# A decoder step on one core: the second mixer's score products 128 keys wide instead of 64

## The chip, the cores and the metric

The kernel runs on one core of one Trainium2 chip. The metric is the device time of one execution in microseconds (us): 1040.94 us, the median of three runs (1039.25 to 1043.57). The engines are TensorE (PE for its matmuls, PEld for its weight loads), VectorE (DVE), ScalarE (ACT), GpSimd (POOL) and SyncE (SP), which issues the DMAs. TensorE runs at one of two clock levels, 1.2 or 2.4 GHz; the profile gives it as a share of full speed.

## The reference

One inference step of a two-layer decoder: 256 prompt tokens and 8 sample tokens, 1024 channels. In each layer four recurrent mixers run side by side, then cross attention, then a feed-forward block. The change touches only the second mixer (HGRN2), and only its prompt part. For each of four heads of 64 channels it computes, in chunks of 64 tokens:

```
b     = cumsum(log_f)                     # per channel, along the tokens
A_ts  = sum_k q[t,k] * exp(b[t,k] - b[s,k]) * k[s,k]     for s <= t, else 0
o     = A @ v  +  (q * exp(b)) @ S        # S is the state carried over chunks
```

The decay between query t and key s is a product of the forget gates of all tokens between them, and it differs per channel.

## The kernel before

Nearly all of TensorE's work is dense projections: `dense` (L294 to L296) multiplies 264 token columns by 128x128 weight blocks in a split precision, three products a block: wh by xh, wh by xl, wl by xh. Weights come from HBM as 512 KB tiles `raw` on SP's queue; ACT makes `wh` (L230), DVE makes `wl` (`sub`, recorded at L92). TensorE takes its instructions in the order that the tile scheduler gave them; the mixers' small products are woven between the dense ones: the mixers are generators, each `yield` hands over to the next one, and one dense projection is put in between by the pace `PACE`.

In `hgrn` keys `hk` (K) and queries Q (a tile of the projection's, `PH` in the profile) lie with channels on the partitions: two heads share the 128 partitions (the halves `HS`: partitions 0 to 63 and 64 to 127), and `i` runs over four pairs of head pair and 128-token half. The matrix A is built in levels w = 1, 2, 4, 8, 16, 32. At level w the keys of each even block of w tokens meet the queries of the odd block that follows it. The key and query rows are scaled in place from level to level (two `mul`, `hk<-hk,hpr` and `PH<-PH,hpr`), so a product at level w already holds the right decays. `quads` issues the products (L740): for each of 4 `i`, 2 blocks of 64 keys (`a`) and 2 heads (`e`), one matmul of 64 keys by 32 queries, contracted over 64 channels. It thus lies in a quarter of the 128x128 array, 64 rows by 64 columns, and the four of one `i` lie in four different quarters. Each float32 matmul is two matmul records in the profile, each with its own weight load: 32 records a level. Before the levels `quads` makes the diagonal with 64 by 64.

The results of head `e` go to the PSUM buffer `ps[e]` (tag `pb`, two buffers, both in use at once). A masked copy on DVE (`copy_predicated`, L763, mask `h{w}`) puts those that belong to the level into `hAc`, 64 tokens wide; the diagonal is a `mul` with `h0`. After the levels `cross` (L772) makes the step across 64 (keys 0 to 63 by queries 64 to 127, 8 products of 64 by 64), and the final tiles `hAt` (one a head, 128 keys by 4 by 128 queries) are put together: a `memset` on DVE (L793), and six copies on ACT (L794, L796). The products with `hAt` (L814) give the output.

Of the kernel before, what the change touches and what calls it, by code (L numbers as in the profile page):

```python
# [10 lines left out]
U32 = mybir.dt.uint32  # L11
# [4 lines left out]
DEPTH, DM, TP, NB, NT = 2, 1024, 256, 8, 264  # L16
# [16 lines left out]
def build_consts():  # L33
    p = np.arange(128)
    cols, off, n = [], {}, 0

    def add(name, a):
        nonlocal n
        a = np.asarray(a, np.float32).reshape(128, -1)
        off[name] = (n, a.shape[1])  # L40
        n += a.shape[1]
        cols.append(a)

    add("ident", np.eye(128))
    add("blk64", (p[:, None] // 64) == (p[None] // 64))
    t64 = np.arange(64)
    s64 = (p % 64)[:, None]
    add("msi", np.concatenate([t64[None] > s64, t64[None] >= s64], 1))
    add("mh", np.stack([(p // 32) % 2 == 0, (p // 32) % 2 == 1], 1))
    t32 = np.arange(32)  # L50
    s32 = (p % 32)[:, None]
    add("id32", t32[None] == s32)
    for w in (1, 2, 4, 8, 16):
        add(f"inv{w}", ((t32[None] // w) % 2 == 1) & (s32 // w == t32[None] // w - 1))
    add("h0", t64[None] == s64)
    for w in (1, 2, 4, 8, 16, 32):
        t = t64[t64 // w % 2 == 1][None]
        add(f"h{w}", s64 // w == t // w - 1)
    add("mneg", np.where(p[None] >= p[:, None], 0.0, -1e30))
    add("pick", (p % 32)[:, None] == np.arange(4)[None])  # L60
    add("eye8", np.broadcast_to(np.eye(8), (128, 8, 8)))
    add("nsc", np.where(p < 32, -2.0, np.where(p < 64, 0.0, -1.0)))
    add("sgn", np.where(p >= 64, -1.0, 1.0))
    return np.ascontiguousarray(np.concatenate(cols, 1)), off


CONSTS, COFF = build_consts()


def body(tc, A, O, depth=DEPTH):  # L70
    nc = tc.nc
    V, S, P, PE = nc.vector, nc.scalar, nc.gpsimd, nc.tensor
# [18 lines left out]
    def tt(out, a, b, op):  # L91
        return V.tensor_tensor(out, a, b, op=op)  # L92

    def mul(out, a, b):
        return tt(out, a, b, ALU.mult)

    def add(out, a, b):
        return tt(out, a, b, ALU.add)
# [19 lines left out]
    def T(tag, shape, name, dt=F32):  # L118
        return wk.tile(list(shape), dt, tag=tag, name=name, bufs=NBUF[tag])

    def psum(tag, shape, name="pm"):
        return psp.tile(list(shape), F32, tag=tag, name=name, bufs=PBUF[tag])

    def tiny(shape, name, bufs=1):
        return wk.tile(shape, F32, tag=name, name=name, bufs=bufs)

    class Stream:
# [5 lines left out]
        def s2(self, name, shape=(128, 2, NT)):  # L133
            return T(self.big, shape, name)
# [7 lines left out]
        def pst(self, shape, name="pm"):  # L142
            return psum(self.ps, shape, name)
# [34 lines left out]
    for _ in range(WARM):  # L178
        ps = psum("pc", [128, 128], "warm")
# [5 lines left out]
    def C(name):  # L185
        o, n = COFF[name]
        return cst[:, o:o + n]

    ident, blk64 = C("ident"), C("blk64")
# [3 lines left out]
    HS = [slice(0, 64), slice(64, 128)]  # L193
# [477 lines left out]
    def hgrn(l, pv, PH):  # L671
        s2, s1, h5, pst, headsum = SB.s2, SB.s1, SB.h5, SB.pst, SB.headsum
        q, f, iv, g = PH
# [48 lines left out]
        def rows(src, t):  # L722
            S.copy(t, turned(pst, src))
            return t
# [1 line left out]
        yield  # L726
        Vr = rows(iv, s2("hVr", [128, 2, 256]))
        yield
        Ac = s2("hAc", [128, 2, 4, 64])
        K = kx[:, :, 0:TP]  # L730
        Q = f[:, :, 0:TP]

        def quads(cols, n):

            ps = [pst([128, 4, n]) for _ in HS]
            for i in range(4):
                for a, as_ in enumerate(HS):
                    t0 = i % 2 * 128 + a * 64
                    for e, hs in enumerate(HS):
                        PE.matmul(ps[e][as_, i, :], lhsT=K[hs, i // 2, t0:t0 + 64], rhs=cols(hs, i // 2, t0),  # L740
                                  start=True, stop=True)
            return ps

        ps = quads(lambda hs, j, t0: q[hs, j, t0:t0 + 64], 64)
        mul(Q, q[:, :, 0:TP], fx[:, :, 0:TP])
        for e in range(2):
            mul(Ac[:, e], ps[e], C("h0")[:, None, :].to_broadcast([128, 4, 64]))
        tw, prod, o = fx[:, :, 0:TP], T("B", [128, 2 * NT], "hpr"), 0
        for w in (1, 2, 4, 8, 16, 32):
            yield  # L750
            ng = TP // (2 * w)
            halves = lambda t: t.rearrange("p j (g two w) -> p j g two w", two=2, w=w)
            ps = quads(lambda hs, j, t0: Q[hs, j, t0:t0 + 64].rearrange("p (g two w) -> p g two w", two=2, w=w)[:, :, 1], 32)
            tv = tw.rearrange("p j (g two) -> p j g two", two=2)
            tn = prod[:, o:o + 2 * ng].rearrange("p (j g) -> p j g", j=2)
            o += 2 * ng
            mul(tn, tv[:, :, :, 0], tv[:, :, :, 1])
            for t, c in ((K, 0), (Q, 1)):
                mul(halves(t)[:, :, :, c], halves(t)[:, :, :, c],
                    tv[:, :, :, 1 - c, None].to_broadcast([128, 2, ng, w]))  # L760
            by = lambda t: t.rearrange("p c (g w) -> p c g w", w=w)
            for e in range(2):
                V.copy_predicated(Ac[:, e].rearrange("p c (g two w) -> p c g two w", two=2, w=w)[:, :, :, 1],  # L763
                                  by(C(f"h{w}")[:, None]).to_broadcast([128, 4, 32 // w, w]).bitcast(U32), by(ps[e]))
            tw = tn

        def cross():
            ps = pst([128, 4, 64])
            for i in range(4):
                t0 = i % 2 * 128  # L770
                for hs in HS:
                    PE.matmul(ps[hs, i, :], lhsT=K[hs, i // 2, t0:t0 + 64], rhs=Q[hs, i // 2, t0 + 64:t0 + 128],  # L772
                              start=True, stop=True)
            return ps

        yield
        if l == 0:
            held.append(Q[:, 0, 0:1])
        psD = cross()
        n = TP // 128  # L780
        qv = Q.rearrange("p j (n two w) -> p j n two w", two=2, w=64)
        kv = K.rearrange("p j (n two w) -> p j n two w", two=2, w=64)
        tv = tw.rearrange("p j (n two) -> p j n two", two=2)
        tn = tiny([128, 2, n], "htw64")
        mul(kv[:, :, :, 0], kv[:, :, :, 0], tv[:, :, :, 1:2].to_broadcast([128, 2, n, 64]))
        mul(qv[:, :, :, 1], qv[:, :, :, 1], tv[:, :, :, 0:1].to_broadcast([128, 2, n, 64]))
        mul(tn, tv[:, :, :, 0], tv[:, :, :, 1])
        tw = tn
        yield
        Kr = rows(K, q.rearrange("p j t -> p (j t)")[:, 0:2 * TP].rearrange("p (c d) -> p c d", c=2))  # L790
        At = [s2("hAt", [128, 4, 128]) for _ in HS]
        for e, hs in enumerate(HS):
            V.memset(At[e][64:128, :, 0:64], 0.0)  # L793
            S.copy(At[e][0:64, :, 64:128], psD[hs])  # L794
            for as_ in HS:
                S.copy(At[e][as_, :, as_], Ac[as_, e])  # L796
        yield
        psG = pst([128, 4, 64])
        for i in range(4):
# [11 lines left out]
        for i in range(4):  # L811
            j, c = i // 2, i % 2
            for h, hs in enumerate(HS):
                PE.matmul(psO[hs, i, :], lhsT=Vr[:, c, j * 128 + h * 64:j * 128 + h * 64 + 64], rhs=At[h][:, i, :],  # L814
                          start=True, stop=c == 0)
# [662 lines left out]
    def layer(l):  # L1478
# [97 lines left out]
        def chain_b():  # L1576
            yield from hgrn(l, pv, PH)
            for _ in d_ml:
                pass
            yield from mlstm(l, pv, PQ, sp, y)  # L1580
# [97 lines left out]
    g = PVL[0]["final_norm_g"]  # L1678
# [7 lines left out]
    t = [SA.s2("y") for _ in range(4)]  # L1686
# [130 lines left out]
```

## Time and profile before

| | |
|---|---|
| median of three runs | 1040.94 us |
| the profiled execution's own time | 1044.91 us |
| its span, first to last instruction | 1043.1 us |
| TensorE busy | 1026.8 us, 98% |
| VectorE busy | 791.7 us, 76% |
| ScalarE busy | 630.5 us, 60% |
| mean granted TensorE clock | 0.988 |

The span is what the profile covers; 1.8 us of the execution lie around it. The profiled execution is 4.0 us longer than the median of the others. A busy share is an average over stages; which engine bounds a stage is read from the waits in it. The mixers of the first layer run from about 25 to 230 us, those of the second from about 540 to 740 us.

### The profile page before, as it was taken

The numbers are of one execution on the slowest core, as the hardware profiler recorded it, in microseconds if no ns is written. First come the engines' busy times: TensorE is split into PE (matmuls) and PEld (weight loads), VectorE is DVE, ScalarE is ACT, GpSimd is POOL, SyncE is SP. The second block draws the span as 40 slices with busy tenths as digits, with TensorE's granted clock in tenths as the row PEclk, the third lists the DMA queues.
The fourth block names the chain that finished last, engine by engine and source line by source line (L and its number), as shares of the span: only waits on it lengthen the run. The fifth ranks groups of instructions, "written<-read, shape, count | busy, mean of one in ns | idle before, by whom it ended". The sixth has DMA issues, their size and how long they took to land.

```text
span 1043.1 us, 26569 instructions
## 1 busy us (share of the span) xinstructions
PE 1026.8 (98%) x10522; PEld 967.6 (93%) x10522; DVE 791.7 (76%) x1766; ACT 630.5 (60%) x1345; POOL 43.4 (4%) x71
## 2 busy tenths in 40 slices
PE   9999999999999999999999999999999999999996
PEld 8999899989879999999999999998988899999996
DVE  7989587688578777868669776876886787777763
ACT  7865456476457766644569354746664577775443
POOL 0000000002002000000010000000020020000000
PEclk9999989999999999999999999999999999999998
DMA  8664267588884566678654433756969655667782
GB/s 283 187 205 125 86 152 232 191 285 281 296 306 154 180 182 182 186 240 289 219 179 153 140 119 116 214 191 210 325 197 340 233 180 179 180 177 225 224 261 79
DMA packets 81580, 213.42 MB, mean 205 GB/s; under 512 B 16432, under 2 KB 19120, under 8 KB 81456
## 3 DMA queue, kind: packets, MB, share of 16 engines
q1 hardware_dynamic: 81456, 211.72, 63.6%
q8 instruction: 83, 1.36, 0.5%
q14 instruction: 41, 0.34, 0.1%
HBM read 195.81 MB, written 15.87 MB: 203 GB/s over the span
## 4 chain that ended last, share of the span: by engine, by line
PE 93%; DVE 4%; ACT 2%; issue 1%; DMA 0%; POOL 0%; DVEq 0%; SPq 0%; ACTq 0%
PE pd L294 21%; PE pd L296 20%; PE pd L295 20%; PE pm L1365 3%; PE pd L307 3%; PE pd L309 2%; PE pd L308 2%; PE pd L1318 2%; PE pd L1319 1%; DVE wl L92 1%; PE pm L1454 1%; PE pd L1320 1%; PE pm L344 1%; PE pm L149 1%; PE pm L1429 1%
## 5 line engine op out<-in xcount | busy, mean ns | idle before, releaser
L230 ACT CAST wh<-raw 128x512 fp32r<-128x512 f32 x544 | 335.9, 619 | 264.0 <-PE pd L295 224.2
L92 DVE TENSOR_TENSOR wl<-raw,wh 128x512 fp32r<-128x512 f32 x544 | 379.1, 700 | 140.0 <-ACT wh L230 125.9
L294 PE MATMUL pd<-xh,wh 128*128 128x264 f32 x1136 | 332.9, 293 | 0.2 <-ACT xh L89 0.2
L295 PE MATMUL pd<-xl,wh 128*128 128x264 f32 x1136 | 326.6, 287 | 0.4 <-DVE xl L110 0.4
L296 PE MATMUL pd<-xh,wl 128*128 128x264 f32 x1136 | 326.4, 287 | 0.2 <-DVE wl L92 0.2
L294 PEld LDWEIGHTS pd<-xh,wh 128*128 128x128 f32 x1136 | 216.5, 191 | 6.4 <-issue 2.2
L296 PEld LDWEIGHTS pd<-xh,wl 128*128 128x128 f32 x1136 | 217.1, 191 | 1.5 <-DVE wl L92 1.1
L295 PEld LDWEIGHTS pd<-xl,wh 128*128 128x128 f32 x1136 | 216.7, 191 | 1.0 <-DVE xl L110 0.6
L294 PE MATMUL pd<-hid,wh 128*128 128x264 f32 x512 | 145.9, 285 | 0.0
L295 PE MATMUL pd<-hid,wh 128*128 128x264 f32 x512 | 145.6, 284 | 0.0
L296 PE MATMUL pd<-hid,wl 128*128 128x264 f32 x512 | 145.6, 284 | 0.0
L295 PEld LDWEIGHTS pd<-hid,wh 128*128 128x128 f32 x512 | 96.6, 189 | 0.0
L296 PEld LDWEIGHTS pd<-hid,wl 128*128 128x128 f32 x512 | 96.4, 188 | 0.0
L294 PEld LDWEIGHTS pd<-hid,wh 128*128 128x128 f32 x512 | 96.3, 188 | 0.0
L107 POOL TENSOR_TENSOR nacc<-nacc,nsq 128x264 f32<-128x264 f32 x41 | 36.7, 896 | 934.4 <-ACT nsq L89 654.7
L92 DVE TENSOR_TENSOR xT<-xT,pd 128x264 f32<-128x264 f32 x80 | 34.0, 424 | 14.2 <-PE pd L309 8.2
L110 DVE SCALAR_TENSOR_TENSOR fft<-pd,rstd 128x264 f32<-128x264 f32 x64 | 27.7, 432 | 15.2 <-PE pd L296 14.2
L1319 PE MATMUL pd<-wl,mgh 128*128 128x256 f32 x128 | 36.5, 286 | 1.3 <-DVE wl L92 1.3
L294 PE MATMUL pd<-mgh,wh 128*128 128x256 f32 x128 | 37.3, 291 | 0.0
L308 PE MATMUL pd<-ol,wh 128*128 128x264 f32 x128 | 37.2, 291 | 0.0
L307 PE MATMUL pd<-oh,wh 128*128 128x264 f32 x128 | 36.7, 289 | 0.5 <-ACT oh L1413 0.5
L1318 PE MATMUL pd<-wh,mgh 128*128 128x256 f32 x128 | 36.7, 292 | 0.0
(551 smaller groups left out, 1777.9 us busy)
## 6 DMA issues: line engine op xcount, KB each, us to landing
raw<-in_ff SPq DMA_DIRECT2D x128, 512.0 KB, 4.3
raw<-in_w_in SPq DMA_DIRECT2D x63, 512.0 KB, 3.7
KV<-in_ck SPq DMA_DIRECT2D x64, 256.0 KB, 5.3
KV<-in_cv SPq DMA_DIRECT2D x64, 256.0 KB, 4.9
raw<-in_wk SPq DMA_DIRECT2D x16, 512.0 KB, 3.5
raw<-in_wv SPq DMA_DIRECT2D x16, 512.0 KB, 4.7
raw<-in_w_out SPq DMA_DIRECT2D x16, 512.0 KB, 4.7
raw<-in_wq SPq DMA_DIRECT2D x16, 512.0 KB, 4.9
```

The lines of the kernel that those rows point to most:

```text
L92: return V.tensor_tensor(out, a, b, op=op)
L107: return P.tensor_tensor(out, a, b, op=ALU.add)
L110: return V.scalar_tensor_tensor(out, in0=a, scalar=s, in1=b, op0=op0, op1=op1, **kw)
L230: S.copy(h, src)
L294: PE.matmul(ps, lhsT=wh, rhs=x, start=i * 8 + k == 0, stop=False)
L295: PE.matmul(ps, lhsT=wh, rhs=y, start=False, stop=False)
L296: PE.matmul(ps, lhsT=wl, rhs=x, start=False, stop=i * 8 + k == n - 1)
L307: PE.matmul(ps, lhsT=wh, rhs=h[k], start=k == 0, stop=False)
L308: PE.matmul(ps, lhsT=wh, rhs=lo[k], start=False, stop=False)
L1318: PE.matmul(ps[m], lhsT=x[:, ms], rhs=wh[:, k % 2], start=first, stop=False)
L1319: PE.matmul(ps[m], lhsT=x[:, ms], rhs=wl[:, k % 2], start=False, stop=False)
L1365: PE.matmul(ps[g:g + 8, :], lhsT=lhs[:, hh, i, b * 8:b * 8 + 8], rhs=kv[a][hh][:, i], start=b < 2 and i == 0, stop=b >= NB - 2 and i == 1)
```

## The change

`quads` drops the loop over `a`: the stationary operand is now all 128 keys of a half, and one matmul is 128 keys by 64 queries (the odd blocks of 128 tokens), contracted over the 64 channels of its head. It lies in half of the array, 64 rows by all 128 columns. There are 8 matmuls a level instead of 16 (16 records instead of 32). The masks `h{w}` are 128 by 64, so the part of a product that belongs to another block is not copied. The masked copies write straight into the final tiles `At`, with 256 elements a partition instead of 128. The diagonal is 128 by 128 with the identity as its mask, which also writes the zeros. The step across 64 is a seventh level of the loop; `cross`, the two memsets and the six ACT copies a layer go. The constants' DMA grows from 1032 to 1224 columns.

```diff
-    add("h0", t64[None] == s64)
-    for w in (1, 2, 4, 8, 16, 32):
-        t = t64[t64 // w % 2 == 1][None]
-        add(f"h{w}", s64 // w == t // w - 1)
+    for w in (1, 2, 4, 8, 16, 32, 64):
+        t = p[p // w % 2 == 1][None]
+        add(f"h{w}", p[:, None] // w == t // w - 1)
...
-        Ac = s2("hAc", [128, 2, 4, 64])
+        At = [s2("hAt", [128, 4, 128]) for _ in HS]
...
-                for a, as_ in enumerate(HS):
-                    t0 = i % 2 * 128 + a * 64
-                    for e, hs in enumerate(HS):
-                        PE.matmul(ps[e][as_, i, :], lhsT=K[hs, i // 2, t0:t0 + 64], rhs=cols(hs, i // 2, t0),
-                                  start=True, stop=True)
+                t0 = i % 2 * 128
+                for e, hs in enumerate(HS):
+                    PE.matmul(ps[e][:, i, :], lhsT=K[hs, i // 2, t0:t0 + 128], rhs=cols(hs, i // 2, t0),
+                              start=True, stop=True)
...
-            mul(Ac[:, e], ps[e], C("h0")[:, None, :].to_broadcast([128, 4, 64]))
+            mul(At[e], ps[e], ident[:, None, :].to_broadcast([128, 4, 128]))
-        for w in (1, 2, 4, 8, 16, 32):
+        for w in (1, 2, 4, 8, 16, 32, 64):
...
-            ps = quads(lambda hs, j, t0: Q[hs, j, t0:t0 + 64].rearrange("p (g two w) -> p g two w", two=2, w=w)[:, :, 1], 32)
+            ps = quads(lambda hs, j, t0: Q[hs, j, t0:t0 + 128].rearrange("p (g two w) -> p g two w", two=2, w=w)[:, :, 1], 64)
...
-                V.copy_predicated(Ac[:, e].rearrange("p c (g two w) -> p c g two w", two=2, w=w)[:, :, :, 1],
-                                  by(C(f"h{w}")[:, None]).to_broadcast([128, 4, 32 // w, w]).bitcast(U32), by(ps[e]))
+                V.copy_predicated(At[e].rearrange("p c (g two w) -> p c g two w", two=2, w=w)[:, :, :, 1],
+                                  by(C(f"h{w}")[:, None]).to_broadcast([128, 4, 64 // w, w]).bitcast(U32), by(ps[e]))
...
-        psD = cross()
...
-        At = [s2("hAt", [128, 4, 128]) for _ in HS]
-        for e, hs in enumerate(HS):
-            V.memset(At[e][64:128, :, 0:64], 0.0)
-            S.copy(At[e][0:64, :, 64:128], psD[hs])
-            for as_ in HS:
-                S.copy(At[e][as_, :, as_], Ac[as_, e])
```

On TensorE, in the first layer around level w = 4, this stands before (operands as in the profile; x16 is a run of 16 matmuls of one line):

```order
L379 MATMUL pm<-cst,a 128x128 x4
L294 MATMUL pd<-xh,wh 128x264
L295 MATMUL pd<-xl,wh 128x264
L296 MATMUL pd<-xh,wl 128x264
L294 MATMUL pd<-xh,wh 128x264
L295 MATMUL pd<-xl,wh 128x264
L296 MATMUL pd<-xh,wl 128x264
L294 MATMUL pd<-xh,wh 128x264
L740 MATMUL pm<-PH_508,hk 64x32 x16
L295 MATMUL pd<-xl,wh 128x264
```

And the same place of the changed kernel, whose lines stand one or two numbers lower:

```order
L378 MATMUL pm<-cst,a 128x128 x4
L293 MATMUL pd<-xh,wh 128x264
L294 MATMUL pd<-xl,wh 128x264
L295 MATMUL pd<-xh,wl 128x264
L293 MATMUL pd<-xh,wh 128x264
L294 MATMUL pd<-xl,wh 128x264
L295 MATMUL pd<-xh,wl 128x264
L293 MATMUL pd<-xh,wh 128x264
L294 MATMUL pd<-xl,wh 128x264
L738 MATMUL pm<-PH_508,hk 128x64 x8
```

The group of 16 has become a group of 8, one dense matmul later; it is the only place on TensorE where a group stands elsewhere than before. In both layers all 16 groups (the diagonal, the six levels and `cross`, now the seventh level) keep their places between the others.

On DVE, in the second layer from level w = 8 on (`wl` and `PQ` belong to dense projections), before:

```order
L763 COPY_PREDICATED hAc<-cst,pm 128x16x8
L92 TENSOR_TENSOR hk<-hk,hpr 128x2x16x8
L92 TENSOR_TENSOR PH_8241<-PH_8241,hpr 128x2x16x8
L763 COPY_PREDICATED hAc<-cst,pm 128x16x8
L92 TENSOR_TENSOR wl<-raw,wh 128x512
L92 TENSOR_TENSOR PQ_8247<-pd,rstd 128x264
```

And of the change:

```order
L761 COPY_PREDICATED hAt<-cst,pm 128x32x8
L91 TENSOR_TENSOR hk<-hk,hpr 128x2x16x8
L91 TENSOR_TENSOR PH_8178<-PH_8178,hpr 128x2x16x8
L761 COPY_PREDICATED hAt<-cst,pm 128x32x8
L91 TENSOR_TENSOR wl<-raw,wh 128x512
L91 TENSOR_TENSOR PQ_8183<-pd,rstd 128x264
```

The masked copies stand where they stood and take twice the elements; the scaling of keys and queries between them is as before.

## Rows read from the trace of the kernel before

**Rows 1.** The page: engines' busy us, clock by slice, weight DMAs (KB, us to landing).

```profile
PE 1026.8 (98%) x10522; PEld 967.6 (93%) x10522; DVE 791.7 (76%) x1766; ACT 630.5 (60%) x1345; POOL 43.4 (4%) x71
...
PEclk9999989999999999999999999999999999999998
...
raw<-in_w_in SPq DMA_DIRECT2D x63, 512.0 KB, 3.7
```

**Rows 2.** Waits of PE: who, for what, us in total, times, longest.

```profile
PE pm L571 <- issue: 2.4, 1, 2.4
```

**Rows 3.** Stretches: length; busy us of PE, PEld, DVE, ACT, POOL; clock, DMA.

```profile
78.00:90.00 12.00, 11.86 (x216) 11.22 (x210) 12.00 (x36) 6.20 (x15) 0.00 (x0) 1.00 0.46 137
...
606.00:622.00 16.00, 16.00 (x335) 15.14 (x335) 11.88 (x34) 8.70 (x19) 0.00 (x0) 1.00 0.36 111
```

**Rows 4.** PE's timeline: start, us, tile, shape, records; two groups, each with its successor.

```profile
608.55 0.67 PE L740 MATMUL pm<-PH,hk 64*64 64x32 f32 x32
609.14 0.39 PE L294 MATMUL pd<-xh,wh 128*128 128x264 f32 x1
...
621.19 0.68 PE L772 MATMUL pm<-PH,hk 64*64 64x64 f32 x16
621.80 0.39 PE L294 MATMUL pd<-xh,wh 128*128 128x264 f32 x1
```

**Rows 5.** PE's timeline: groups of other weight widths and columns, each with its successor.

```profile
60.35 2.03 PE L344 MATMUL pm<-rRV,SWT 64*64 64x2 f32 x64
62.31 0.39 PE L294 MATMUL pd<-xh,wh 128*128 128x264 f32 x1
...
69.25 1.09 PE L534 MATMUL pm<-AR,a 64*64 64x128 f32 x16
70.28 0.29 PE L322 MATMUL pm<-cst,vec 128*48 128x128 f32 x1
...
162.47 1.06 PE L1187 MATMUL pm<-lgw,lKr 128*128 128x4 f32 x8
163.46 0.69 PE L1178 MATMUL pm<-lKr,lVg 128*64 128x64 f32 x14
...
181.74 0.92 PE L1221 MATMUL pm<-PQ,PQ 64*128 64x256 f32 x8
182.59 0.44 PE L859 MATMUL pm<-cst,RT 128*128 128x128 f32 x2
```

**Rows 6.** Line 1187's matmuls: duration in ns, min/median/max, first and last start.

```profile
L1187 PE MATMUL pm<-lgw,lKr x16: 252/253/273, 162.5 to 675.7; 128*128 128x4 f32 x16
```

**Rows 7.** Groups by shape: count, busy us, mean ns of one, idle before.

```profile
L763 DVE COPY_PREDICATED hAc<-cst,pm 128x128 f32<-128x128 uint32 x24 | 7.4, 349 | 0.9 <-PE pm L740 0.8
L92 DVE TENSOR_TENSOR M<-pm,cst 128x512 f32<-128x512 f32 x8 | 5.5, 685 | 1.9 <-PE pm L534 1.9
L92 DVE TENSOR_TENSOR hAc<-pm,cst 128x256 f32<-128x256 f32 x4 | 1.5, 414 | 0.0
L793 DVE MEMSET hAt<- 64x256 f32 x4 | 1.1, 272 | 0.4
...
L796 ACT COPY hAt<-hAc 64x256 f32<-64x256 f32 x8 | 3.2, 404 | 1.2 <-DVE hAc L763 1.0
```

**Rows 8.** Timeline of DVE, then of PE, around level w = 4, second layer.

```profile
603.61 0.44 DVE L763 COPY_PREDICATED hAc<-cst,pm 128x128 f32<-128x128 uint32 x1
...
604.55 0.43 DVE L763 COPY_PREDICATED hAc<-cst,pm 128x128 f32<-128x128 uint32 x1
...
604.78 1.00 PE L740 MATMUL pm<-PH,hk 64*64 64x32 f32 x32
605.71 0.39 PE L294 MATMUL pd<-xh,wh 128*128 128x264 f32 x1
```

**Rows 9.** Two stretches of the first layer, columns as in rows 3.

```profile
117.00:119.30 2.30, 0.00 (x0) 0.00 (x0) 0.00 (x0) 0.00 (x0) 0.00 (x0) 1.00 0.15 39
119.70:123.10 3.40, 3.40 (x16) 2.75 (x17) 0.00 (x0) 1.60 (x3) 0.00 (x0) 0.50 0.02 5
```

More of the change, by code (lines that the diff above doesn't have):

```diff
@@ L736, in quads @@
             for i in range(4):
-                for a, as_ in enumerate(HS):
-                    t0 = i % 2 * 128 + a * 64
-                    for e, hs in enumerate(HS):
-                        PE.matmul(ps[e][as_, i, :], lhsT=K[hs, i // 2, t0:t0 + 64], rhs=cols(hs, i // 2, t0),
-                                  start=True, stop=True)
+                t0 = i % 2 * 128
+                for e, hs in enumerate(HS):
+                    PE.matmul(ps[e][:, i, :], lhsT=K[hs, i // 2, t0:t0 + 128], rhs=cols(hs, i // 2, t0),
+                              start=True, stop=True)
             return ps
-        ps = quads(lambda hs, j, t0: q[hs, j, t0:t0 + 64], 64)
+        ps = quads(lambda hs, j, t0: q[hs, j, t0:t0 + 128], 128)
         mul(Q, q[:, :, 0:TP], fx[:, :, 0:TP])
         for e in range(2):
-            mul(Ac[:, e], ps[e], C("h0")[:, None, :].to_broadcast([128, 4, 64]))
+            mul(At[e], ps[e], ident[:, None, :].to_broadcast([128, 4, 128]))
         tw, prod, o = fx[:, :, 0:TP], T("B", [128, 2 * NT], "hpr"), 0
-        for w in (1, 2, 4, 8, 16, 32):
+        for w in (1, 2, 4, 8, 16, 32, 64):
             yield
@@ L762, in hgrn @@
             for e in range(2):
-                V.copy_predicated(Ac[:, e].rearrange("p c (g two w) -> p c g two w", two=2, w=w)[:, :, :, 1],
-                                  by(C(f"h{w}")[:, None]).to_broadcast([128, 4, 32 // w, w]).bitcast(U32), by(ps[e]))
+                V.copy_predicated(At[e].rearrange("p c (g two w) -> p c g two w", two=2, w=w)[:, :, :, 1],
+                                  by(C(f"h{w}")[:, None]).to_broadcast([128, 4, 64 // w, w]).bitcast(U32), by(ps[e]))
             tw = tn
[L767 to L776, printed above, removed]
         if l == 0:
             held.append(Q[:, 0, 0:1])
-        psD = cross()
[L780 to L788, printed above, removed]
         yield
         Kr = rows(K, q.rearrange("p j t -> p (j t)")[:, 0:2 * TP].rearrange("p (c d) -> p c d", c=2))
-        At = [s2("hAt", [128, 4, 128]) for _ in HS]
-        for e, hs in enumerate(HS):
-            V.memset(At[e][64:128, :, 0:64], 0.0)
-            S.copy(At[e][0:64, :, 64:128], psD[hs])
-            for as_ in HS:
-                S.copy(At[e][as_, :, as_], Ac[as_, e])
         yield
```

## The prediction

> **What bounds the kernel now.** Start with the page: TensorE (PE) is busy 1026.8 of 1043.1 us [rows 1], so only 16.3 us of the whole span are idle, and a gain or a loss elsewhere counts only if it reaches PE. Next read PE's waits: the longest is a single stop of 2.4 us [rows 2] in which PE waited for nothing that the profile shows. Then take the stretches where the second mixer's levels lie. In the first layer's 78 to 90 us PE is busy 11.86 of 12.00 and DVE 12.00; in the second's 606 to 622 us PE 16.00 of 16.00, DVE 11.88 and ACT 8.70 [rows 3]. There PE runs one instruction after the other, dense products around small ones. So what the change does to PE's own time there lengthens or shortens the kernel by the same amount; DVE matters only through a delay, above all at the start, where it has no slack; ACT does not matter.
>
> **What one group costs PE now.** I take start to next start, so that the array's switch between tile sizes is included. A level of 32 records (16 products of 64 keys by 32 queries, four quarters of the array side by side, so 8 rounds) takes 609.14 - 608.55 = 0.59 us; the cross step, 16 records of 64 by 64 queries, two quarters side by side, so also 8 rounds, takes 0.61 [rows 4]. Half the records and twice the columns, yet the same time: neither the count of instructions nor the columns set it. What is the same in both is the round's weights, 64 columns wide. L344 says so too: 64 records with 2 columns each, 32 rounds of two, take 1.96 us [rows 5]. With a fixed part S and a round p: 32p + S = 1.96 and 8p + S = 0.60 give p = 0.057 us and S = 0.15 us. A round lasts 0.057 us with 2, 32 or 64 moving columns: it waits for its weights of 64 columns.
>
> **What it costs then.** The new product has 128 weight columns and 64 moving ones; two (the two heads) lie side by side, so a level is again 8 rounds. For weights of 128 columns with hardly any moving ones there is L1187: 8 records, one after the other, 4 columns each, take 0.99 us [rows 5]; less S that is 0.105 us a round, and from its duration, (1.06 - 0.253) / 7, it is 0.115 [rows 5, 6]. That is twice the 0.057 of 64 columns. Do two such loads run side by side? L1221 is the same tile as the new one (64 rows, 128 columns, heads alternating): 8 records, two rounds of 256 and two of 128 columns, 0.85 us. L534 gives the price of moving columns: 8 rounds of 128 columns, 1.03 us, so 0.110 a round, 0.220 for 256. Two of each and S are 0.81; one product after the other would be 1.47. They run side by side [rows 5].
>
> So a new group is 8 x (0.105 to 0.115) + 0.15 = 0.99 to 1.07, I take 1.02, against 0.60: **+0.42 us a group**. The diagonal has 128 moving columns, 0.110 a round, and comes out the same; its old form had 32 records of 64 by 64 in four quarters, 8 rounds, 0.60. There are 8 groups a layer (the diagonal, six levels, the cross step that is now the seventh level), 16 in all: 16 x 0.42 = **+6.7 us**. From below: if a round stayed at 0.057 (64 moving columns alone need 0.055, half of L534's), only the two diagonals would grow, by 8 x 0.053 each: +0.9. From above: rounds that load and multiply in turn, 0.112 + 0.055 = 0.167 with 64 columns and 0.222 with the diagonal's 128: 14 x (1.49 - 0.60) + 2 x (1.93 - 0.60) = +15.
>
> The row's verdict can be set against a rule. The Trainium skill, "TensorE: Matmul & The Clock Gate", section "The mechanism", says that a weight load overlaps products in flight only where the row group differs. By it the next pair's weights could not load under this pair's products, and the sum would be the upper end just worked out. Here L772 speaks against it: by that rule its group would be 8 x (0.057 + 0.055) + 0.15 = 1.05, and it is 0.61 [rows 4].
>
> **DVE.** The masked copies go from 24 of 128 elements, 0.349 us each, to 28 of 256. The trace has no such copy of 256; a product from PSUM takes 0.414 with 256 and 0.685 with 512 elements [rows 7], so 128 more cost 0.135 (bounds: nothing, if the fixed part is all, and 0.27), and I take 0.484. That is 28 x 0.484 - 24 x 0.349 = +5.2; the four diagonal products go from 0.414 to 0.685, +1.1; the four memsets, 1.1 in all, go. Sum +5.2 us over both layers. Nearly all of it lies beside PE, which is itself 6.7 longer in the same stretches; in 78 to 90 us DVE gets about +0.5 for the diagonal and 6 x 0.135 for three levels, 1.3, and PE there four groups, 1.7, so the copies still fit. If that cover were gone, 5.2 us would be the price.
>
> One place is not covered. At level w = 4 PE's group follows the previous one after a few dense products and takes 605.71 - 604.78 = 0.93 instead of 0.59: its second head waits for the PSUM buffer until the second copy of level w = 2 is done (604.55 + 0.43 = 604.98) [rows 8]. Behind it queue the dense products. Two longer copies lie ahead of that release, 2 x 0.135 = 0.27 a layer: **+0.5 us** over both (0 to 1.1). In the first layer one dense matmul now stands ahead of the group, which can only shorten this wait.
>
> **The rest.** The six ACT copies a layer (0.404 each for four of them [rows 7]) end long before L814 needs their tiles, and ACT is half idle: 0. The seventh level brings one pair of copies behind the scaling of the keys, whose transposes stand a dense projection later: 0. The constants' DMA has 98 KB more ahead of weight tiles on SP's queue, a fifth of a tile that lands in 3.7 us [rows 1], 0.7 us; PE's list of waits has none for a DMA, so 0, and 0.7 if that cover is gone.
>
> **Sum.** +6.7 + 0.5 = +7.2 us. On the profiled execution's own time, 1044.91 us (span 1043.1 and 1.8 around it), that is 1052.1. This execution lies 4.0 us above the median of 1040.94, perhaps by the stop below; on the median the sum is 1048.1, and I forecast 1048 us.
>
> **Rivals.** A, a round stays at 0.057, since two row halves load one under the other: +0.9 + 0.5, 1042.3 us. For it: no row shows 128-column weights in two halves with as few as 64 moving columns. Against: L1187 and the doubling from 64 to 128.
>
> B, on the other side: the count of PE's instructions decides. A level's 0.45 us without S is 0.0141 a record; with half the records twelve levels lose 0.225 each, -2.7, the diagonals still need +0.9. And the stop: from 117.0 to 119.3 us no engine does anything, in the middle of a group of 64 tiny products, and then PE runs at the lower clock level, 1.2 GHz (0.50), for 3.4 us [rows 9], 1.7 lost, part of the first dip in the page's clock line [rows 1]. If PE lacks instructions there, the 224 fewer of them a layer (112 products and 112 loads) could end it, -4.1. Together -5.9: 1035.0 us. It decides if a level's group takes clearly less than 0.59. Against: 16 records of L772 take as long as 32 of L740 [rows 4]. The Trainium skill, "TensorEngine Tiling (Array Packing)", section "Instruction Overhead", speaks for it: about 60 cycles a matmul whatever its columns. An estimate by it, 25 ns at 2.4 GHz, makes 0.8 us of the old level; the trace has 0.59.
>
> C, the forecast's PE cost, but the stop falls away since the instructions stand elsewhere, and the median holds it: 1048.1 - 4.1 = 1044 us. For: nothing in the profile explains the stop; against: the second layer has the same code and no such stop.
>
> D, load and product in turn: +15 + 0.5, 1056.4 us.
>
> **Chances.** Forecast 0.66, A 0.12, B 0.05, C 0.11, D 0.06. A measurement of this kernel tells 0.5%, 5.2 us, from no change: faster is below 1035.7, slower above 1046.1. Faster: B, 0.05. Same: A, C and the forecast's lower edge, 0.26. Slower: the rest, 0.69. The range 1042 to 1053 holds the forecast with its bounds (0.99 to 1.07 a group and 0 to 1.1 of waiting make 1047.2 to 1049.6, and the runs themselves spread by 4.3), A and C; B and D are left out.
>
> **What would show it.** PE's groups of the new line: about 1.02 us from start to next start, 16 records each; at 0.60 it is A, below 0.5 B, near 1.5 D. The copies at 256 elements near 0.48 us, the group at w = 4 some 0.27 longer than the others plus the 0.34 it waits now, all else in these stretches unchanged and PE still without idle time. The forecast is wrong if the groups don't lengthen, or if they do and the end doesn't move with them.

## The result, and the profile after

The changed kernel takes 1056.57 us (median of four runs, 1053.78 to 1058.74) against 1042.26 of the kernel before beside it (four runs): a ratio of 1.013, interval 1.0098 to 1.0162. That is slower, as forecast, but by 14.3 us instead of 7.2, and outside the range.

The profiled execution has a span of 1056.8 us and a mean granted clock of 0.984. Its page, engines and clock by slice:

```profile
PE 1038.3 (98%) x10298; PEld 977.2 (92%) x10298; DVE 799.3 (76%) x1766; ACT 625.5 (59%) x1333; POOL 43.7 (4%) x71
...
PEclk9989889999999999999999999999999999999998
```

TensorE is busy 11.5 us longer with 224 matmul records less [rows 1]. The levels of the second mixer, PE's timeline (columns as in [rows 4]): the diagonal and w = 4 in the first layer, then w = 4 and w = 8 in the second, each with its successor.

```profile
81.64 1.16 PE L738 MATMUL pm<-PH,hk 64*128 64x128 f32 x16
82.73 0.39 PE L293 MATMUL pd<-xh,wh 128*128 128x264 f32 x1
...
94.38 1.64 PE L738 MATMUL pm<-PH,hk 64*128 64x64 f32 x16 [0.23 <-DVE hAt L761]
95.95 0.40 PE L295 MATMUL pd<-xh,wl 128*128 128x264 f32 x1
...
616.23 1.70 PE L738 MATMUL pm<-PH,hk 64*128 64x64 f32 x16 [0.19 <-DVE PH L91]
617.86 0.39 PE L293 MATMUL pd<-xh,wh 128*128 128x264 f32 x1
...
620.68 1.11 PE L738 MATMUL pm<-PH,hk 64*128 64x64 f32 x16
621.72 0.39 PE L293 MATMUL pd<-xh,wh 128*128 128x264 f32 x1
```

The group that took 0.59 from 608.55 on [rows 4] is now 621.72 - 620.68 = 1.04. PE is as full as before (columns as in [rows 3]):

```profile
601.00:620.00 19.00, 18.81 (x191) 17.51 (x190) 16.48 (x39) 7.21 (x15) 0.00 (x0) 1.00 0.28 89
620.00:636.00 16.00, 16.00 (x274) 15.06 (x273) 11.88 (x32) 6.39 (x13) 0.00 (x0) 1.00 0.39 120
```

In PE's waits a row has come that the kernel before has not: the second one, sums over `lsq` in another mixer (L148, `headsum` of the mLSTM).

```profile
PE pm L738 <- issue: 2.2, 1, 2.2
PE pm L148 <- ACT lsq L88: 1.8, 2, 1.3
PE pd L1291 <- DVE wl L91: 1.3, 4, 0.5
```

Of its 1.8 us, 1.3 lie in the second layer and 0.5 in the first.

The stop of [rows 2] is still there, at another place: it has moved from L571 into the group of the seventh level, and a stretch at the lower clock follows it as it did in [rows 9].

```profile
112.55 0.88 PE L738 MATMUL pm<-PH,hk 64*128 64x64 f32 x10
115.64 0.90 PE L738 MATMUL pm<-PH,hk 64*128 64x64 f32 x6 [2.22 <-issue]
```

```profile
116.00:122.00 6.00, 6.00 (x33) 5.72 (x31) 2.14 (x5) 0.69 (x2) 0.00 (x0) 0.51 0.12 20
```

The DVE's groups by shape (columns as in [rows 7]):

```profile
L761 DVE COPY_PREDICATED hAt<-cst,pm 128x256 f32<-128x256 uint32 x28 | 13.8, 526 | 2.8 <-PE pm L738 2.8
...
L91 DVE TENSOR_TENSOR hAt<-pm,cst 128x512 f32<-128x512 f32 x4 | 2.6, 682 | 0.2 <-PE pm L738 0.2
```

The copies are at 0.526 (forecast 0.484), the diagonal's product at 0.682 (0.685).

### The profile page after: what moved, and what is told of

Read it like the earlier page. It is cut to its first block, busy times and chain, and to the rows that moved or that the text cites. A ratio compares the mean times of both kernels' runs of the same rounds, so it can differ in the third digit from the quotient of the medians.

```text
span 1056.8 us, 26111 instructions
## 1 busy us (share of the span) xinstructions
PE 1038.3 (98%) x10298; PEld 977.2 (92%) x10298; DVE 799.3 (76%) x1766; ACT 625.5 (59%) x1333; POOL 43.7 (4%) x71
## 3 DMA queue, kind: packets, MB, share of 16 engines
q8 instruction: 81, 1.33, 0.5%
## 4 chain that ended last, share of the span: by engine, by line
PE 90%; DVE 4%; ACT 2%; DMA 2%; issue 1%; POOL 0%; SPq 0%; DVEq 0%; ACTq 0%
PE pd L293 21%; PE pd L295 20%; PE pd L294 20%; PE pm L1337 3%; PE pd L306 3%; PE pd L308 2%; PE pd L307 2%; DVE wl L91 2%; PE pm L738 1%; PE pm L1426 1%; PE pm L343 1%; PE pd L1291 1%; PE pm L1401 1%; PE pd L1290 1%; PE pm L148 1%; PE pd L1292 1%
## 5 line engine op out<-in xcount | busy, mean ns | idle before, releaser
L109 DVE SCALAR_TENSOR_TENSOR fft<-pd,rstd 128x264 f32<-128x264 f32 x64 | 27.7, 433 | 15.4 <-PE pd L295 14.3
```

Of the source, the lines that this page charges most:

```text
L109: return V.scalar_tensor_tensor(out, in0=a, scalar=s, in1=b, op0=op0, op1=op1, **kw)
```

## The experiments

A run's time has two parts that move on their own: the work, and the time that the granted clock takes away. So beside the medians I use span times mean granted clock, the **time at full clock**, as a mean over a kernel's runs with its standard error; span less that is what the lower clock cost. The kernel before ran beside each of the three groups of experiments, 25, 28 and 31 times. At full clock it came to 1030.05, 1030.0 and 1030.3, each ± 0.2, so the groups can be set against each other there; 10.9 to 11.9 us were lost to the clock.

Theories, as the expectations name them: W, the weights' width makes PE's groups longer; C, the longer copies on DVE hold PE up (not the prediction's rival C); K, more time at the lower clock; F, the change shifts where in the program PE's instructions are fetched from memory, and a fetch that falls badly delays something. The trace counts these fetches as a queue of its own, 81 packets of 1.33 MB together after (83 before), 16 KB each. The 20,596 matmuls and weight loads over 81 are 254 a packet; with PE's semaphore instructions it is 256, which the part on the stop shows below.

**The change again.** No edit.

> The changed kernel once more, for a second profile and a sharper ratio. Theory W (the weights of 128 columns cost 0.43 us in each of 16 groups and longer waits at w = 4, 8.6 us in all as the first trace shows; the rest of the 14 us is where the clock's dips and two waits happened to fall): the ratio comes out nearer 1.009 than 1.013, the groups are again 1.03 us, but the dips lie elsewhere. Rival K (the new groups themselves bring more time at the lower clock): again some 14 us, with more time at the lower clock than the kernel before has. Rival C (the longer copies on VectorE make PE wait): PE's waits on VectorE sum to some us.

Measured: 1056.52 us, ratio 1.0112 (1.0088 to 1.0137). At full clock 1041.35 ± 0.31: the change costs 11.35 ± 0.4 of work; lost to the clock 13.2 ± 1.1, some 1.3 to 2 (± 1.2) more than before. K alone is out, and is at most a small part. C is no large part either, since PE waits 0.2 us for the copies here. W alone expected 8.6 us and falls 2.7 short.

**Quarters instead of halves.** Products 64 keys by 64 queries (the diagonal 64 by 128), four to a row, everything else as in the change:

```diff
-                    PE.matmul(ps[e][:, i, :], lhsT=K[hs, i // 2, t0:t0 + 128], rhs=cols(hs, i // 2, t0),
-                              start=True, stop=True)
+                    for as_ in HS:
+                        PE.matmul(ps[e][as_, i, :], lhsT=K[hs, i // 2, t0 + as_.start:t0 + as_.stop],
+                                  rhs=cols(hs, i // 2, t0), start=True, stop=True)
```

> The change with the products cut back to weights of 64 keys: 16 products a level of 64 keys by 64 queries, four quarters side by side, the same results in the same places; copies, tiles and the seventh level as in the change. Theory W: a level's group is back at about 0.60 us (the diagonal 1.03, as it moves 128 columns), the gain on the change is 14 x 0.43 = 6 us or a little more, and the time lies some 2 us above the kernel before, 1044 us. Rival C: the copies are as long as in the change, so the time stays near 1056. Rival K: like W in time, but the time at the lower clock falls with it.

Measured: 1045.64, ratio 1.0013 (0.9992 to 1.0034); 1034.0 ± 0.3 at full clock, 7.3 under the change (W expected 6 or a little more). Level w = 4 in the first layer, then w = 8 in the second with its successor, on PE:

```profile
92.52 1.70 PE L739 MATMUL pm<-PH,hk 64*64 64x64 f32 x32 [1.88 <-DVE hAt L762]
...
610.48 0.69 PE L739 MATMUL pm<-PH,hk 64*64 64x64 f32 x32
611.11 0.39 PE L293 MATMUL pd<-xh,wh 128*128 128x264 f32 x1
```

Twice the columns of [rows 4] at the same weight width: 0.63 instead of 0.59. At twice the width: 1.04. So W holds for the groups: the width sets it, and rival A is out. The first row shows what cost the copies have where PE is not lengthened to match: a wait of 1.88 at w = 4, in the one place that the prediction called uncovered. The 4.0 us that are left against the kernel before are not accounted for in full. The time lost to the clock is lower too, 9.3 ± 0.9, as K would have it; but the change shifted by 192, below, loses only 7.9 with the wide groups, so the width isn't what sets it.

**Half of the copies.** The change, with masked copies of the first two of four pairs only (half of the off-diagonal part of A is left out):

```diff
-                V.copy_predicated(At[e].rearrange(...)[:, :, :, 1], by(C(f"h{w}")[:, None]).to_broadcast([128, 4, 64 // w, w])..., by(ps[e]))
+                V.copy_predicated(At[e].rearrange(...)[:, 0:2, :, 1], by(C(f"h{w}")[:, None]).to_broadcast([128, 2, 64 // w, w])..., by(ps[e][:, 0:2]))
```

> The change with masked copies of 128 elements instead of 256 (only the pairs of the first two heads of each copy; the other half of A stays diagonal, so part of the computation is left out); products as in the change. Theory W: groups stay at 1.03 us, the wait at w = 4 loses some 0.3 us a layer: 0.5 to 1 us faster than the change, 1055. Rival C: the copies were the cause, so most of the 14 us goes, under 1048.

Measured: 1049.23, ratio 1.0048 (1.0023 to 1.0073); 1036.7 ± 0.55 at full clock, 4.65 under the change. Both theories miss: W expected 1055, C under 1048. The group at w = 4 gets a little back, 609.53 - 608.18 = 1.35 instead of 1.63 in the second layer and 1.26 instead of 1.57 in the first:

```profile
608.18 1.42 PE L738 MATMUL pm<-PH,hk 64*128 64x64 f32 x16
609.53 0.39 PE L295 MATMUL pd<-xh,wl 128*128 128x264 f32 x1
```

Together 0.6. The profile has no stop of PE for "issue" any more, which is 2.2 of the rest, though PE has as many instructions as in the change, in the same order but for the two groups at w = 4, one dense product earlier each; so the stop hangs on more than the count of what stands ahead of it. The remainder, some 1.8, is not accounted for.

**Before, again.** No edit.

> The kernel before, unchanged, profiled a second time: how much its own executions differ. Theory W: spans differ by some 4 us from one execution to the next by where the dips of the clock and the one stop of PE fall; ratio 1.000. Rival K: its time at the lower clock is the same in every execution.

Measured: 1042.6, ratio 0.9977 (0.9955 to 0.9999); 1029.85 ± 0.19. This is what equality looks like here: the interval just misses 1 for the same kernel, so a ratio of 0.998 means nothing.

**The same programs, their instructions shifted.** Tiny products of 32 by 32 with one column are put at the kernel's start, in exchange for warm-up products (`k` of them, `WARM` fewer; a product is two matmuls and two loads), so that all that follows stands 192 PE instructions later in the changed kernel, and 64, 32, 96, 128 or 160 later in the kernel before:

```diff
+    ps = psum("pc", [128, 128], "pad")
+    for i in range(k):
+        g = slice(32 * (i % 4), 32 * (i % 4) + 32)
+        PE.matmul(ps[g, i:i + 1], lhsT=ones[g, 0:32], rhs=ones[g, 0:1], start=True, stop=True)
```

> The change with 192 more PE instructions at the start (50 tiny products in place of two warm-up products), so that the blocks of 256 instructions in which PE's program is fetched begin, at the end of the second layer's mixers, at the same place of the program as in the kernel before. Theory F (a fetch of 16 KB meets the copy of the memory values to HBM there; the copy's issue on SyncE takes 1.8 us instead of 0.4, its read-back comes late, ScalarE waits for it and PE waits for ScalarE at the sums over lsq): that issue is back at 0.4 us, PE's wait at lsq in the second layer goes, span times mean clock falls by 1.4 to 2.4 us against the change. Rival C (the mixers' chain is itself late by the longer copies): the wait at lsq stays.

Measured: 1047.53, ratio 1.0055 (1.0031 to 1.0078); 1038.3 ± 0.34 at full clock, lost to the clock 7.9 ± 0.6. The same work on the same data, with 192 instructions added, is 9 us faster than the change by the medians (6 by the ratios to the kernel before, run beside each): 3.05 ± 0.5 of work, 5.3 ± 1.3 of clock. The wait for `lsq` in the second layer is gone (0.4 is left in the first). But PE's stop for "issue" has also shrunk, from 2.2 in the change (2.5 in its repetition) to 0.6. By the profiles wait and stop together are 2.9 to 4.3 us, so the 3.05 are not the price of the wait alone.

> The kernel before with 64 more PE instructions at the start (17 tiny products in place of one warm-up product): at the end of the second layer's mixers the blocks of 256 lie as in the change. Theory F: the issue of the memory values' copy takes some 1.4 to 1.8 us and PE waits at lsq by 1 to 2 us more, though nothing of the mixer is changed; span times mean clock 1031 to 1032 instead of 1030. Rival C: no wait at lsq, 1030.

Measured: 1039.95, ratio 0.9986 (0.9964 to 1.0009); 1030.8 ± 0.25, lost 8.1. The kernel before, with its mixer untouched, now has the change's wait:

```profile
PE pm L149 <- ACT lsq L89: 2.1, 1, 2.1
```

The time rises by only 0.8 ± 0.35, because the stop is nearly gone here (0.2 and 0.3 instead of 2.4): this run shows the wait, not its price.

The chain behind it is read from SyncE's timeline (start, us the issue took, line, what). In the kernel before, the copy of the memory values to HBM (`kvd`) and their read-back (`KVm`):

```profile
711.17 0.42 SPq L1327 DMA_DIRECT2D kvd<-mv  x1
711.69 0.40 SPq L276 DMA_DIRECT2D raw<-in_wv  x1
712.18 0.41 SPq L1355 DMA_DIRECT2D KV<-in_ck  x1
714.29 0.33 SPq L1343 DMA_DIRECT2D KVm<-kvd  x1
```

In the change:

```profile
723.20 1.75 SPq L1299 DMA_DIRECT2D kvd<-mv  x1
725.05 0.38 SPq L275 DMA_DIRECT2D raw<-in_wv  x1
725.52 0.40 SPq L1327 DMA_DIRECT2D KV<-in_ck  x1
727.32 0.33 SPq L1315 DMA_DIRECT2D KVm<-kvd  x1
```

In the change shifted by 192:

```profile
713.67 0.42 SPq L1303 DMA_DIRECT2D kvd<-mv  x1
714.18 0.39 SPq L279 DMA_DIRECT2D raw<-in_wv  x1
716.76 0.33 SPq L1319 DMA_DIRECT2D KVm<-kvd  x1
```

In the kernel before shifted by 64:

```profile
701.54 0.42 SPq L1331 DMA_DIRECT2D kvd<-mv  x1
702.06 2.09 SPq L280 DMA_DIRECT2D raw<-in_wv  x1
704.24 0.38 SPq L1359 DMA_DIRECT2D KV<-in_ck  x1
705.93 0.33 SPq L1347 DMA_DIRECT2D KVm<-kvd  x1
```

One issue of 0.4 us takes longer, the copy's own (1.75) or, not as expected, the one behind it (2.09), and in the DMA records a fetch of PE's instructions begins beside it: at 723.2 in the change, at 702.1 in the shifted kernel before. Where no issue is long, the fetches next to the copy lie elsewhere: 703.9 and 715.7 in the kernel before, with its copy at 711.17; 705.4 and 717.9 in the change shifted by 192. What follows is read from the ScalarE's waits. Change, before, before shifted by 64, change shifted by 192, in this order (us in all, times, longest):

```profile
ACT stmp L229 <- DMA KVm<-kvd: 6.6, 2, 3.7
```

```profile
ACT stmp L230 <- DMA KVm<-kvd: 4.4, 2, 2.3
```

```profile
ACT stmp L234 <- DMA KVm<-kvd: 6.3, 2, 4.6
```

```profile
ACT stmp L233 <- DMA KVm<-kvd: 4.9, 2, 2.8
```

ScalarE waits longer for the read-back, `lsq` is behind that on its queue, and PE waits for `lsq`. On PE, the change and then the change shifted by 192:

```profile
734.96 1.16 PE L148 MATMUL pm<-lsq,cst 128*128 128x264 f32 x4 [1.30 <-ACT lsq L88]
```

```profile
723.96 1.05 PE L148 MATMUL pm<-lsq,cst 128*128 128x264 f32 x4
```

The thirteen profiles hold this first copy of the memory values twice each, once a layer. All 26, in us:

| profile, layer | longest issue from the copy to the read-back | PE's nearest fetch begins, after the copy's issue | copy's issue to read-back's | PE's wait for `lsq` |
|---|---|---|---|---|
| change, second | 1.75 | 0.02 | 4.12 | 1.30 |
| change again, second | 1.85 | 0.07 | 4.07 | 2.42 |
| quarters, second | 1.39 | 0.09 | 3.62 | 0.60 |
| half of the copies, second | 1.57 | -0.04 | 3.77 | 1.81 |
| before shifted by 64, second | 2.09 | 0.56 | 4.39 | 2.14 |
| before shifted by 160, first | 1.78 | 0.34 | 4.15 | 1.99 |
| the other 20 | 0.40 to 0.42 | over 1.3 before or 3.8 behind | 2.66 to 3.20 | 0 to 0.77 |

So a fetch at this copy and a late read-back go together without exception. Waits up to 0.8 come without one. Over all DMAs of the thirteen profiles, 134 of 8073 issues on SyncE took more than 1 us, and 126 of these began within 0.5 us of a fetch of PE's; of all issues 9% did.

**Narrow products and narrow diagonal.** The quarters with the diagonal 64 by 64 too, the final tiles zeroed by GpSimd, shifted by 192:

```diff
+            P.memset(At[e], 0.0)
...
-            mul(At[e], ps[e], ident[:, None, :].to_broadcast([128, 4, 128]))
+            for as_ in HS:
+                mul(At[e][as_, :, as_], ps[e][as_], ident[as_, None, as_].to_broadcast([64, 4, 64]))
```

> The quarters again (weights of 64 keys, 64 queries a product, copies straight into the final tiles, seventh level), the diagonal of 64 by 64 with the final tiles zeroed by GpSimd, and 192 PE instructions at the start. Theory W with F: all 16 groups at 0.60 us, no late issue, what is left is the longer copies' wait at w = 4: span times mean clock 1030 to 1032, the time equal to the kernel before within 0.3%. Rival C: 1034 as with the quarters, or more.

Measured: 1046.83, ratio 1.0038 (1.0018 to 1.0057); 1032.0 ± 0.55 at full clock, 12.8 lost. At full clock that is the upper end of what W with F expected; the time misses the equality within 0.3% by a little. The profile has the same wait as the quarters, about as long as the 2.0 of work:

```profile
94.26 1.69 PE L743 MATMUL pm<-PH,hk 64*64 64x64 f32 x32 [2.09 <-DVE hAt L769]
```

So the longer copies do hold PE up where its groups are short (C), and in the change itself, with the longer products, the wait there is 0.23.

**Shifts of the kernel before by 32, 96, 128 and 160.**

> The kernel before with 32 more PE instructions at the start (10 tiny products in place of one warm-up product). Theory F, that the two stops of PE (2.4 us in the first layer, 1 to 2.4 at lsq in the second) come from where the fetches of PE's program fall: each shift has either, both or neither, and span times mean clock takes values between 1027.5 (neither) and 1032 (both) though the work is the same; where the first stop is missing the time lost to the lower clock is near 8 us instead of 11. Rival (the stops are chance of an execution, not of the shift): all shifts give 1030.

The run has nine tiny products: 9 x 4 instructions, less the 4 of the warm-up product, are the 32.

> As the shift by 32, with 96 (25 tiny products in place of one warm-up product). Theory F: at lsq a fetch comes a little earlier than with 64, before the copy of the memory values, so no wait there; 1027.5 if the first stop is missing too. Rival: 1030.

> As the shift by 32, with 128 (34 tiny products in place of two warm-up products). Theory F: no fetch at the copy of the memory values, no wait at lsq; 1027.5 or 1030 by the first stop. Rival: 1030.

> As the shift by 32, with 160 (42 tiny products in place of two warm-up products). Theory F: no wait at lsq; 1027.5 or 1030 by the first stop. Rival: 1030.

| shift | median us | ratio, interval | at full clock | lost to the clock |
|---|---|---|---|---|
| 32 | 1041.52 | 0.999 (0.997 to 1.001) | 1028.5 ± 0.27 | 11.65 |
| 96 | 1039.76 | 0.9972 (0.9949 to 0.9994) | 1028.8 ± 0.4 | 9.7 |
| 128 | 1045.44 | 1.0012 (0.9986 to 1.0039) | 1031.0 ± 0.26 | 11.9 |
| 160 | 1041.3 | 0.9976 (0.9956 to 0.9997) | 1029.7 ± 0.5 | 9.6 |

The same work differs by 2.5 us at full clock between the shifts 32 and 128, which the errors don't explain, nor the start: the first dense product begins at 5.91 and 6.08 us (6.09 unshifted). The 1027.5 that F expected of a good shift was not reached. In the second layer the shifts by 96, 128 and 160 have no `lsq` wait, as expected. The shift by 160 has one of 2.0 in the first layer, where none was expected; the table above shows a fetch at the copy there. F holds as a mechanism, but I could not foretell from the count alone where a fetch falls. None of the kernels run beats the kernel before by more than can be told from none.

## Why the prediction came out wrong

**A group on PE: right.** Forecast 1.02 (0.99 to 1.07); measured 1.04 at w = 2, 8 and 16 (+0.44 to +0.45) and 1.05 to 1.13 at w = 32 and the seventh level (+0.41 to +0.49). B (faster than 0.59) and D (1.49) are out, and so is A. Two kinds of group were mis-sized: the diagonal and w = 1. Before, their first products started while the preceding group of L534 was still going, which has the same tile form, 64 by 64, and the two cost 1.46 to 1.49 together; now L738 begins when L533 has ended, and the two cost 2.06 to 2.12. That is +0.60 to +0.63 instead of 0.42, some +0.75 over four groups.

**The wait at w = 4: right.** The group grew by 0.70 in both layers (1.57 against 0.87, and 1.63 against [rows 8]'s 0.93), forecast 0.42 + 0.27 = 0.69. The dense product that now stands ahead of it in the first layer shortened nothing.

**DVE: right to call it covered, as far as waits show.** The copies cost 0.526 a piece, inside the bounds, which makes DVE's sum +6.3 instead of +5.2, and PE shows no new wait for them but 0.23. The 1.8 us of the half copies that nothing accounts for leave room for a small part of theirs. The quarters say what the cover is worth: 1.9 us in the first layer alone.

Summed over the 16 groups from start to next start that is +8.3 by the second layer's rows (4.1 for its eight) against the forecast 7.2.

**The rest at 0: this is the step that failed.** It listed what the change removes and adds, found each hidden, and did not ask what else depends on the number of PE's instructions. The change issues 224 fewer in each layer's mixer (112 products and 112 loads), so the second layer's tail comes 448 earlier in the count, and a fetch (there is one every 256 instructions) lands beside the copy of the memory values. That is the wait for `lsq` in the second layer: 1.3 us in the change's profile, 2.4 in its repetition, none in the kernel before. The sign "PE still without idle time" failed with it. The shift experiments show the cause from both sides: gone when the change is shifted, present when the unchanged kernel is. The first layer's 0.4 to 0.5 have no fetch at the copy; their cause is open. With the groups' 8.3 the waits for `lsq` make 10.1 to 11.1 of the 11.35 ± 0.4 found at full clock. From the forecast 1048.1 to 1056.57 it is 8.5 us: 1.1 more for the groups, 1.8 to 2.8 of `lsq`, 1.3 to 2 of clock, 1.3 by which the kernel before was itself slower beside the change (1042.26). Some 1 to 3 us have no name.

**The stop: rival C's premise failed, the sum's did not.** It moved with the change (L571, 117.0 to 119.3 before; 113.4 to 115.6 after), at nearly the same price, so it takes no part in the difference. The prediction left open what it is; the traces tell. In the DMA records a fetch begins at 117.06 before and at 113.41 after, at the moment PE stops; the fetch before it lies 8.4 and 14.8 us back. Counted in the order of their starts (matmuls, weight loads and semaphore instructions), 3009 of PE's instructions lie ahead of the stop before and 2241 after: both are a multiple of 256 and 193 more. The thirteen profiles have thirteen stops for "issue" of over 0.2 us. At twelve the count is a multiple of 256 and 193 more, and PE goes on 2.2 to 2.4 us after its last fetch began, however long it had stopped. So PE had come to the end of a block of 256 whose successor was not there, and the stop is as long as that fetch was late. With half of the copies, where there is no stop, PE passes the same count at 111.4, and the fetch had begun 3.9 us before. The thirteenth (0.6 us, before shifted by 128) stands at another count.

**The base.** The median of three, 1040.94, was 1.8 to 2.8 below what 25 to 31 runs of the same kernel gave (1042.76 to 1043.75). The range of 1042 to 1053 stood on it.

**Open.** Some 1.3 to 2 us (± 1.2) of the change lie in the lower clock. In both profiles of the change a group ahead of the changed part, L533, runs at 0.50 in each layer:

```profile
71.05:72.95 1.90, 1.90 (x17) 1.57 (x16) 0.04 (x1) 0.00 (x0) 0.00 (x0) 0.50 0.73 246
...
593.14:595.05 1.91, 1.91 (x18) 1.58 (x18) 0.10 (x1) 0.00 (x0) 0.00 (x0) 0.50 0.76 169
```

The unchanged kernel's repetition shows it at the first of the two places, at 69.83, so it is not the change's alone. In the thirteen profiles 44 stretches at 0.50 lie ahead of the kernel's end. Each begins within 2 us behind tiny products (L344, L571 and L578 in the kernel before, 64 in a row) or in or right behind a wait or stop of PE of 1.9 us or more. At the four stops of 1.9 to 2.5 us the clock fell each time, for 3.4 or 6.8 us; at the shorter ones it didn't. That fits the shifted change, whose stop is short, losing less; but the profiles of one kernel differ in the other places, and no experiment tells why the shifts of 64 and 192 lose 8 us to the clock and others 12. Why a fetch comes late enough to stop PE is also open. Moving the copy of the memory values to another engine's queue would test the chain more directly; it wasn't tried, because the scheduler then orders PE's tail anew, just where the wait lies.

## What to carry to other kernels

On an engine that is full, price a product by the width of its weights and by its neighbours on the array: here the same form behind the same form overlapped, and another form did not. In this kernel up to 2.5 us hang on where the instruction fetches fall; before crediting or blaming an edit with 2 us or so, shift the unchanged kernel by a handful of instructions and see what that does. Take the base from more than three runs.

## What the runs showed of the hardware that was not expected

- TensorE's program came in blocks of 16 KB, one for 256 of its instructions, by DMA. At the end of a block PE went on only 2.2 to 2.4 us after the next one's fetch had begun (twelve stops). A DMA issue of SyncE at the copy of the memory values took 1.39 to 2.09 us beside such a fetch, instead of 0.33 to 0.42.
- Two loads of 128 columns in the two row halves went side by side at about the 0.11 us a round of a single one ((1.04 - 0.15) / 8); halving the width halved it to 0.06, whatever the columns, 32 or 64.
- Products of one tile form in different tiles flowed into each other over the boundary of two groups (1.46 for the pair); products of another form began only at the end, for 0.6 more.
